# Where the sums of squares of x are made, and when their roots reach the tokens

## The chip, the cores and the metric

One core of a Trainium2 chip runs one program. The metric is the device time of one execution in microseconds (us), the lower the better. The engines have these short names: PE (TensorE, matrix products; PEld is its weight load), DVE (VectorE), ACT (ScalarE), POOL (GpSimd), SP (SyncE, which here issues most transfers). Results of PE land in PSUM, which has eight banks; everything else works in SBUF.

## The reference, cut to what matters

The kernel computes one decoder layer on 528 tokens (16 meta tokens and 512 of the sequence) of width 2048:

```
xn = x * rsqrt(mean(x * x) + eps) * g_pre        # one root for each token
p  = xn @ w_in                                   # q | k | v | z | r | h | b | c | z_conv
log_a = log_sigmoid(r @ w_gate_up + b_gate) / 16
y_gla  = rmsnorm(gated linear attention of q, k, v, log_a) * silu(z)
y_conv = b * conv3(c * h) * silu(z_conv)
out = x + rmsnorm(concat(y_gla, y_conv) @ w_out)
```

What the change concerns is the first line and the first columns of the second: q, k and r. The root of a token multiplies every column of that token, so a product may be made on x times g_pre alone, and its result multiplied by the root afterwards. The kernel calls the root's reciprocal `rstd` and keeps it spread over all 128 partitions, one column for each token.

## The kernel before, in words

Tokens are columns: x lies as 16 blocks (`kt`) of 128 features by 528 tokens, the tokens in two halves of 264 (8 meta tokens and 256 others each). A product in full fp32 accuracy is made of parts: each operand is split into a rounded high part and the low rest, and three matmuls (high by high, high by low, low by high) are added up in PSUM. ACT makes the high parts (a copy), DVE the low ones (a subtraction).

The kernel has these stages:

- **Load and first products.** x arrives in nine pieces (`XCUT`: two single blocks, then seven pairs). For each block ACT makes the high part (L670) and DVE the low part (L671), times g_pre. ACT also squares each piece. The first two squares go to the two planes of `acc`, the seven later pairs to one of two buffers `sqs`, and DVE adds them to `acc` (L696). Weights of k head 0 and q head 0 come in granules of eight blocks, split by L145 and L146. PE walks through the blocks: six matmuls for k, six for q (`plain_k`), four for r in each. Each of r, k and q has two banks, one for each half of the tokens.
- **rstd.** After step `kt == 10` in the code, PE adds the squares over partitions with a matrix of ones (fp32, two halves by two planes), which leaves the sum of each token on every partition. ACT takes the root (L711), DVE the reciprocal of 528 columns (L712). Then DVE scales r, k and q (`normal`, L723), and r is split into `rr` (L763 to L765), which the decay of head 0 and later ones reads.
- **Plain products** of v0, v1, z0 and z1 (`do_plain`), on x without its root, each 16 steps of six matmuls, two banks each, weights from three buffers for the high and three for the low parts. Beside them DVE makes `xn`, x times g_pre times rstd (`normalise`, L776, 16 instructions), and from it sums and differences of quarter blocks (`combine`, L783), split by L788 and L789 (`block`).
- **Fast products.** All other products go in pairs of column tiles by seven products of quarter blocks (`Pair`, order P5, P1, P6, P2, P3, P7, P4), with weights combined by L200 and L230 and split by L124 and L125, two ahead of PE. The attention's stages, the convolution and the output product follow in the same manner.

The order of the code is the order of priority: a planner walks through the code with its own costs, and puts an instruction into its engine's queue when its operands are ready by that reckoning, the earlier line first. Later lines can be drawn forward where an engine would have nothing to do. Each queue then runs strictly in that order on the chip.

The names that the text uses: `st` are the banks of the sums by ones, `warm` a bank that eight matmuls at the very start write and nobody reads, `scr` the tile that holds `acc`, `sqs` and small raw inputs, `ini` the pool of the first stage, `ident` a unit matrix, `HM` (after) the eight meta tokens of a half.

Of the kernel before, what the change touches and what calls it, by code (L numbers as in the profile page):

```python
# [9 lines left out]
F32 = mybir.dt.float32  # L10
F32R = mybir.dt.float32r
U32 = mybir.dt.uint32
AF = mybir.ActivationFunctionType
ALU = mybir.AluOpType

P = 128
D = 2048
KT = D // P
NM = 16
S = 512  # L20
L = NM + S
H = 4
DV = 256
RANK = 16
RU = 6 * RANK
HI = 4 * RANK
CH = 64
NP = S // P
# [3 lines left out]
XHALF = L // 2  # L32
# [13 lines left out]
def hymba_kernel(ctx, tc, xT, x, g_pre, w_r, w_t, w_up, b_gate, g_gla, w_conv, w_o, g_post, out):  # L46
# [10 lines left out]
    g1 = left.enter_context(tc.tile_pool(name="g1", bufs=1))  # L57

    def bank(name):
        return ps.tile([P, 512], F32, tag="bank", name=name)  # L60

    def mm(out_, lhsT, rhs, start, stop, **kw):
        nc.tensor.matmul(out_, lhsT, rhs, start=start, stop=stop, **kw)  # L63

    V, A, G = nc.vector, nc.scalar, nc.gpsimd


    epst = const.tile([P, 1], F32, name="epst")
# [13 lines left out]
    ones = const.tile([P, P], F32, name="ones")  # L82
    G.memset(ones, 1.0)
    ident = const.tile([P, P], F32, name="ident")
# [19 lines left out]
    scr = xp.tile([P, 3 * NB * XHALF], F32, tag="xt1", name="scr")  # L104
# [3 lines left out]
    WQ = 4 * NB * P  # L108
    wr2 = q0w[:, WQ:WQ + KT * 2 * RANK].rearrange("p (k r) -> p k r", r=2 * RANK)
    acc = scr[:, 0:2 * L].rearrange("p (k t) -> p k t", t=L)  # L110
    sqs = [scr[:, L * (2 + 2 * i):L * (4 + 2 * i)].rearrange("p (k t) -> p k t", t=L)
           for i in range(2)]
    wr_raw = scr[:, 6 * L:6 * L + KT * RANK].rearrange("p (k r) -> p k r", r=RANK)
    wup_raw = scr[0:RU, 7 * L:7 * L + H * P]
    r32 = scr[0:2 * RANK, 8 * L:9 * L]

    def raw_x(kt):
        return (xa if kt < NB else xb), kt % NB
# [13 lines left out]
    def new_raw(shape=None):  # L132
        tag = slots.pop(0)
        t = wp.tile(shape or [P, NB, P], F32, tag=tag, name="raw", bufs=1)
        held[id(t)] = (t, tag)
        return t

    def free(t):
        slots.append(held.pop(id(t))[1])
# [9 lines left out]
    def new_gran():  # L149
        return (wp.tile([P, NB, P], F32R, tag="whi", name="whi"),  # L150
                wp.tile([P, NB, P], F32R, tag="wlo", name="wlo"), new_raw())
# [5 lines left out]
        return gran  # L157


    def plain_k(pts, wt, kt, c0):  # L160
        hi, lo = wt[kt // NB][0:2]
        k = kt % NB
        first, last = kt == 0, kt == KT - 1
        xt, xk = raw_x(kt)
        w = XHALF - c0
        for n in range(2):
            mm(pts[n][:, 0:w], hi[:, k, :], xt[0][:, n, xk, c0:], first, False)
        for n in range(2):
            mm(pts[n][:, 0:w], hi[:, k, :], xt[1][:, n, xk, c0:], False, False)
        for n in range(2):  # L170
            mm(pts[n][:, 0:w], lo[:, k, :], xt[0][:, n, xk, c0:], False, last)

    def natural(t):

        return ([(t[:, NM // 2:NM // 2 + XHALF], 0, XHALF)],
                [(t[:, NM // 2 + XHALF:], NM // 2, XHALF), (t[:, 0:NM // 2], 0, NM // 2)])
# [473 lines left out]
    with tc.tile_pool(name="ini", bufs=1, reuse_waits="tile") as ini:  # L650
        tt = ini.tile([P, NB, XHALF], F32, name="tt")
        xr = ini.tile([P, KT, L], F32, name="xr")
        rstd = ini.tile([P, L], F32, name="rstd")

        warm = bank("warm")
        for _ in range(WARM):
            mm(warm[:, 0:P], ones, ones, True, True)
        r_ps = [bank("r0"), bank("r1")]
        k_ps = [bank("k00"), bank("k01")]
        q_ps = [bank("q00"), bank("q01")]  # L660
        q0v = q0w[:, 0:WQ].rearrange("p (g s k c) -> p g s k c", g=2, s=2, k=NB)
        wk = [new_gran(), None]
        wq_ = [(q0v[:, g, 0], q0v[:, g, 1], new_raw()) for g in range(2)]
        for n_, (k0, k1) in enumerate(XCUT):
            ks = slice(k0, k1)
            nc.sync.dma_start(xr[:, ks, :], xT[:, ks, :])
            for kt in range(k0, k1):
                xt, xk = raw_x(kt)
                src = xr[:, kt, :].rearrange("p (s t) -> p s t", t=XHALF)
                A.activation(xt[0][:, :, xk, :], src, AF.Copy, scale=gp[:, kt:kt + 1])  # L670
                V.scalar_tensor_tensor(out=xt[1][:, :, xk, :], in0=src, scalar=gp[:, kt:kt + 1],  # L671
                                       in1=xt[0][:, :, xk, :].bitcast(F32),
                                       op0=ALU.mult, op1=ALU.subtract)
            for a, b in WCUT.get(k0, ()):
                if a == NB:
                    free(wk[0][2])
                    wk[1] = new_gran()
                fill_gran(wk[a // NB], w_t[TILE["k0"]], a, b)
                fill_gran(wq_[a // NB], w_t[TILE["q0"]], a, b)
            if k0 == 0:  # L680
                A.dma_start(wr_raw, w_r)
                V.tensor_copy(wr2[:, :, 0:RANK], wr_raw)
                V.tensor_tensor(out=wr2[:, :, RANK:], in0=wr_raw,
                                in1=wr2[:, :, 0:RANK].bitcast(F32), op=ALU.subtract)
            if k0 == 8:
                nc.sync.dma_start(wup_raw, w_up)
                nc.sync.dma_start(bg, b_gate)
                G.tensor_scalar(out=nbg, in0=bg, scalar1=-1.0, scalar2=None, op0=ALU.mult)
                nc.sync.dma_start(gg, g_gla)
                nc.sync.dma_start(wc, w_conv)  # L690
            if k0 < 2:
                A.activation(acc[:, k0:k1, :], xr[:, ks, :], AF.Square)
            else:
                sq = sqs[n_ % 2]
                A.activation(sq, xr[:, ks, :], AF.Square)
                V.tensor_tensor(out=acc, in0=acc, in1=sq, op=ALU.add)  # L696
        for kt in range(KT):
            xt, xk = raw_x(kt)
            plain_k(k_ps, wk, kt, 0)
            plain_k(q_ps, wq_, kt, NM // 2)  # L700
            for i in range(2):
                for n in range(2):
                    mm(r_ps[n][0:2 * RANK, 0:XHALF], wr2[:, kt, :], xt[i][:, n, xk, :],
                       kt == 0 and i == 0, kt == KT - 1 and i == 1)
            if kt == 10:
                for n in range(2):
                    t = slice(n * XHALF, (n + 1) * XHALF)
                    st_ = bank(f"st{n}")
                    for i in range(2):
                        mm(st_[:, 0:XHALF], ones, acc[:, i, t], i == 0, i == 1)  # L710
                    A.activation(rstd[:, t], st_[:, 0:XHALF], AF.Sqrt, bias=epst, scale=1.0 / D)  # L711
                V.reciprocal(rstd, rstd)  # L712
        for raw in (wk[1][2], wq_[0][2], wq_[1][2]):
            free(raw)

# [3 lines left out]
                        op=ALU.subtract)  # L719
        def normal(dst, pts, c0, rows=slice(0, P)):  # L720
            for n in range(2):
                for o, s, e in dst[n]:
                    V.tensor_tensor(out=o, in0=pts[n][rows, s - c0:e - c0],  # L723
                                    in1=rstd[rows, n * XHALF + s:n * XHALF + e], op=ALU.mult)

        def new_k(h):
            kn[h] = g1.tile([P, L], F32, tag="kn", name="kn")
            return natural(kn[h])

        def new_q(h):  # L730
            qn[h] = g1.tile([P, L], F32, tag="qn", name="qn")[:, 0:S]
            return main_only(qn[h])
# [22 lines left out]
        def want_plain(n):  # L755
            if n in plain and n not in grans:
                grans[n] = [load_gran(n, g) for g in range(2)]

        want_plain("v0")

        normal(natural(r32), r_ps, 0, slice(0, 2 * RANK))
        rr = g1.tile([RU, L], F32R, tag="rr", name="rr")
        A.copy(rr[0:2 * RANK], r32)  # L763
        A.copy(rr[HI:RU], r32)
        V.tensor_tensor(out=rr[2 * RANK:HI], in0=r32, in1=rr[0:2 * RANK].bitcast(F32),  # L765
                        op=ALU.subtract)
        normal(new_k(0), k_ps, 0)
        normal(new_q(0), q_ps, NM // 2)

        xn = xr  # L770
        B = {(i, j): xn[:, NB * i:NB * i + NB, XHALF * j:XHALF * j + XHALF]
             for i in range(2) for j in range(2)}

        def normalise():
            for kt in range(KT):
# [16 lines left out]
        def do_plain(n, then):  # L792
            c0, new = plain[n]
            want_plain(n)
            if then:
                want_plain(then)
            pts = [bank(f"{n}{i}") for i in range(2)]
            for kt in range(KT):
                plain_k(pts, grans[n], kt, c0)
            grans.pop(n)  # L800
            normal(new(int(n[1:])), pts, c0)

# [4 lines left out]
        xt = [xp.tile([P, 3, NB, XHALF], F32R, tag=f"xt{i}", name=f"xt{i}") for i in range(2)]  # L807
# [23 lines left out]
        first = 3  # L831
# [14 lines left out]
    st = {}  # L846
# [223 lines left out]
```

## Time and profile before

| | |
|---|---|
| median of three runs | 819.46 us (818.55 to 820.85) |
| profiled execution | 820.74 us, span 819.0 us |
| granted TensorE clock, mean | 0.991 |
| PE busy | 793.0 us (97%), 6364 matmul instructions |
| DVE busy | 688.0 us (84%) |
| ACT busy | 437.2 us (53%) |
| POOL busy | 11.7 us (1%), 31 instructions |

The span is the time from the first to the last instruction of the profiled execution; its device time is 1.7 us longer. In the rows of the timeline the columns are: start, length (both in us), engine, line, operation, output and inputs by their names in the program, shape, number of instructions in the row, and in brackets the idle time before it with what ended it. A line is that of the helper which issues the instruction; all matmuls have line 63. Fp32 matmuls appear as two records each.

### The profile page before, as it was taken

Reading aid. Unit: us, or ns where it says so; the run is one execution under the profiler, and the core shown is the slowest. Engines: PE = TensorE matmul, PEld = TensorE weight load, DVE = VectorE, ACT = ScalarE, POOL = GpSimd, SP = SyncE. Lnnn points to the kernel's source line nnn. Section 1 sums busy time; section 2 is a strip of 40 time slices with the busy share of each in tenths; the row PEclk is TensorE's granted clock in tenths of the full one; section 3 lists DMA queues with packets and bytes.
Section 4 is the critical chain, followed back from the end, with each engine's and each line's share of the span. In section 5 each row is a group of like instructions: output and inputs, shape, how many; then the busy total and the mean of one; then the engine's idle time right before and its main releaser. Section 6 shows DMA issues by size and latency. Waiting matters only on the chain.

```text
span 819.0 us, 15183 instructions
## 1 busy us (share of the span) xinstructions
PE 793.0 (97%) x6364; PEld 775.8 (95%) x6364; DVE 688.0 (84%) x820; ACT 437.2 (53%) x638; POOL 11.7 (1%) x31
## 2 busy tenths in 40 slices
PE   8999999999999989999999999999999999999992
PEld 8999999999999989999999999999999889999992
DVE  6999979689796798878888878787879986788887
ACT  7635675585867475544444444444447534444442
POOL 0000000000000100000000000000000000000000
PEclk9999999999999999999999999999999999999997
DMA  9612242334224523153333333333333522333346
GB/s 290 222 52 92 93 134 97 104 109 150 76 79 145 164 79 104 69 189 112 119 104 111 104 112 107 111 106 115 102 110 119 171 78 77 103 103 107 100 166 248
DMA packets 33029, 98.99 MB, mean 121 GB/s; under 512 B 4064, under 2 KB 8800, under 8 KB 32320
## 3 DMA queue, kind: packets, MB, share of 16 engines
q1 hardware_dynamic: 28512, 88.44, 33.1%
q10 hardware_dynamic: 3168, 5.38, 1.9%
q0 software_dynamic: 1280, 4.20, 1.5%
q8 instruction: 50, 0.82, 0.4%
q14 instruction: 19, 0.16, 0.1%
HBM read 89.61 MB, written 8.39 MB: 120 GB/s over the span
## 4 chain that ended last, share of the span: by engine, by line
PE 76%; DVE 15%; ACT 3%; issue 3%; DMA 2%; DVEq 0%; SPq 0%; ACTq 0%
PE out L63 5%; PE out1P L63 4%; PE out2P L63 3%; PE out3P L63 3%; PE v L63 3%; DVE wlo L125 3%; PE h0c0P L63 2%; PE v2v3P L63 2%; PE h5c5P L63 2%; PE h2c2P L63 2%; PE h7c7P L63 2%; PE h6c6P L63 2%; PE h4c4P L63 2%; PE h3c3P L63 2%; PE h1c1P L63 2%
## 5 line engine op out<-in xcount | busy, mean ns | idle before, releaser
L124 ACT CAST whi<-raw 128x1024 fp32r<-128x1024 f32 x225 | 235.0, 1050 | 257.8 <-DVE raw L200 87.6
L125 DVE TENSOR_TENSOR wlo<-raw,whi 128x1024 fp32r<-128x1024 f32 x225 | 274.0, 1221 | 63.2 <-ACT whi L124 58.4
L200 DVE TENSOR_TENSOR raw<-raw 128x1024 f32<-128x1024 f32 x75 | 90.3, 1221 | 7.8 <-DMA raw<-in_w_t_dram 7.0
L230 DVE TENSOR_TENSOR raw<-raw 128x1024 f32<-128x1024 f32 x25 | 30.6, 1222 | 0.6
L145 ACT CAST whi<-raw 128x1024 fp32r<-128x1024 f32 (+2 forms) x13 | 10.9, 843 | 19.5 <-PE v L63 12.8
L63 PE MATMUL out<-whi,xt 128*128 128x512 f32 x64 | 20.0, 394 | 0.0
L63 PE MATMUL out3P<-whi,xt 128*128 128x256 f32 x96 | 17.2, 282 | 0.4 <-ACT whi L124 0.4
L63 PE MATMUL out2P<-whi,xt 128*128 128x256 f32 x96 | 17.2, 282 | 0.4 <-ACT whi L124 0.4
L63 PE MATMUL out1P<-whi,xt 128*128 128x256 f32 x96 | 17.1, 281 | 0.0
L63 PEld LDWEIGHTS out3P<-whi,xt 128*128 128x128 f32 x96 | 14.7, 188 | 0.6 <-ACT whi L124 0.6
L63 PEld LDWEIGHTS out2P<-whi,xt 128*128 128x128 f32 x96 | 14.7, 188 | 0.6 <-ACT whi L124 0.6
L63 PEld LDWEIGHTS out<-whi,xt 128*128 128x128 f32 x64 | 12.0, 188 | 2.8
L63 PEld LDWEIGHTS out1P<-whi,xt 128*128 128x128 f32 x96 | 14.7, 188 | 0.0
L63 PE MATMUL out2P<-wlo,xt 128*128 128x256 f32 x48 | 13.4, 280 | 0.0
L63 PE MATMUL out3P<-wlo,xt 128*128 128x256 f32 x48 | 13.4, 280 | 0.0
L63 PE MATMUL out1P<-wlo,xt 128*128 128x256 f32 x48 | 13.4, 280 | 0.0
L63 PE MATMUL out<-wlo,xt 128*128 128x512 f32 x32 | 12.6, 394 | 0.0
L146 DVE TENSOR_TENSOR wlo<-raw,whi 128x1024 fp32r<-128x1024 f32 (+2 forms) x13 | 12.5, 972 | 0.0
L605 DVE SCALAR_TENSOR_TENSOR y<-hh,wc,y 128x512 f32<-128x512 f32 x16 | 12.0, 749 | 0.2
L363 ACT ACTIVATE junk<-y 128x256 f32<-128x256 f32 x18 | 7.5, 418 | 8.7 <-DVE y L474 8.4
L63 PE MATMUL out3P<-whi,xb 128*128 128x256 f32 x64 | 11.7, 282 | 0.0
L63 PE MATMUL out2P<-whi,xb 128*128 128x256 f32 x64 | 11.6, 282 | 0.0
(751 smaller groups left out, 2708.8 us busy)
## 6 DMA issues: line engine op xcount, KB each, us to landing
raw<-in_w_t_dram SPq DMA_DIRECT2D x108, 512.0 KB, 4.0
raw<-in_w_o_dram SPq DMA_DIRECT2D x24, 512.0 KB, 4.0
raw<-in_w_o_dram SPq DMA_DIRECT2D x16, 256.0 KB, 3.6
xres<-in_x_dram SPq DMA_DIRECT2D x4, 1024.0 KB, 8.1
xr<-in_xT_dram SPq DMA_DIRECT2D x7, 528.0 KB, 7.3
z<-zd POOLq DMA_DIRECT2D x8, 256.0 KB, 3.5
yd<-z POOLq DMA_DIRECT2D x8, 256.0 KB, 2.5
yg<-yd SPq DMA_DIRECT2D x1, 2048.0 KB, 8.7
```

The costliest lines, as they stand in the source:

```text
L63: nc.tensor.matmul(out_, lhsT, rhs, start=start, stop=stop, **kw)
L124: A.copy(hi, raw)
L125: V.tensor_tensor(out=lo, in0=raw, in1=hi.bitcast(F32), op=ALU.subtract)
L145: A.copy(hi[:, k, :], raw[:, k, :])
L146: V.tensor_tensor(out=lo[:, k, :], in0=raw[:, k, :], in1=hi[:, k, :].bitcast(F32), op=ALU.subtract)
L200: V.tensor_tensor(out=a, in0=a, in1=b, op=ALU.add)
L230: V.tensor_tensor(out=raw["11"], in0=raw["11"], in1=raw["22"], op=ALU.subtract)
L363: A.activation(junk, oy["src"], AF.Square, accum_out=fin["ssq"][:, t, n:n + 1])
L605: V.scalar_tensor_tensor(out=y, in0=hh[:, i:i + S], scalar=wc[:, j, i:i + 1], in1=y, op0=ALU.mult, op1=ALU.add)
```

## The change

The sums of squares of five of the seven later pairs are added by GpSimd; those of the last two pairs and the two planes are added by DVE, so that one plane is left. A third buffer of squares is there. The roots are no longer made on 128 equal partitions: the squares of 128 tokens are the weights of a matmul with one column of ones, which leaves one sum per token on its own partition (four groups of 128 tokens, two of 8 meta tokens). Root and reciprocal are taken of these six columns, a unit matrix is scaled by them, and a matmul of ones with that diagonal spreads them over all partitions. All of it goes through the bank `warm`. The sums stand in the code after step 3 of v0, the spread after step 8, and scaling r, k and q behind it; splitting r stands after step 1 of v1. In the loop over blocks r goes ahead of k and q, and the two halves of q share a bank.

```diff
-    sqs = [scr[:, L * (2 + 2 * i):L * (4 + 2 * i)].rearrange("p (k t) -> p k t", t=L)
-           for i in range(2)]
+    sqs = [scr[:, L * i:L * (2 + i)].rearrange("p (k t) -> p k t", t=L) for i in (2, 4, 9)]
...
-    def plain_k(pts, wt, kt, c0):
+    def plain_k(pts, wt, kt, c0, shared=False):
...
+        kw = [{}, {"skip_group_check": True} if shared else {}]
         for n in range(2):
-            mm(pts[n][:, 0:w], hi[:, k, :], xt[0][:, n, xk, c0:], first, False)
+            mm(pts[n][:, 0:w], hi[:, k, :], xt[0][:, n, xk, c0:],
+               first and not (shared and n), False, **kw[n])
...
-        q_ps = [bank("q00"), bank("q01")]
+        q_bank = bank("q0")
+        q_ps = [q_bank[:, 0:S // 2], q_bank[:, S // 2:]]
...
-                sq = sqs[n_ % 2]
+                sq = sqs[n_ % 3]
                 A.activation(sq, xr[:, ks, :], AF.Square)
-                V.tensor_tensor(out=acc, in0=acc, in1=sq, op=ALU.add)
+                if k0 < 12:
+                    G.tensor_tensor(out=acc, in0=acc, in1=sq, op=ALU.add)
+                elif k0 == 14:
+                    V.tensor_tensor(out=sq, in0=sq, in1=sqs[(n_ - 1) % 3], op=ALU.add)
+                    V.tensor_tensor(out=acc, in0=acc, in1=sq, op=ALU.add)
+                    V.tensor_tensor(out=acc[:, 0, :], in0=acc[:, 0, :], in1=acc[:, 1, :],
+                                    op=ALU.add)
         for kt in range(KT):
             xt, xk = raw_x(kt)
-            plain_k(k_ps, wk, kt, 0)
-            plain_k(q_ps, wq_, kt, NM // 2)
             for i in range(2):
                 for n in range(2):
                     mm(r_ps[n][0:2 * RANK, 0:XHALF], wr2[:, kt, :], xt[i][:, n, xk, :],
                        kt == 0 and i == 0, kt == KT - 1 and i == 1)
-            if kt == 10:
-                for n in range(2):
-                    t = slice(n * XHALF, (n + 1) * XHALF)
-                    st_ = bank(f"st{n}")
-                    for i in range(2):
-                        mm(st_[:, 0:XHALF], ones, acc[:, i, t], i == 0, i == 1)
-                    A.activation(rstd[:, t], st_[:, 0:XHALF], AF.Sqrt, bias=epst, scale=1.0 / D)
-                V.reciprocal(rstd, rstd)
+            plain_k(k_ps, wk, kt, 0)
+            plain_k(q_ps, wq_, kt, NM // 2, True)
+        HM = NM // 2
+        inv = ini.tile([P, NP + 2], F32, name="inv")
+        diag = ini.tile([P, NP, P], F32, name="diag")
+        diam = ini.tile([HM, 2, HM], F32, name="diam")
+        col = [n * XHALF + HM + t * P for n in range(2) for t in range(2)]
+
+        def token_sums():
+            o = warm[:, 0:NP + 2]
+            for t in range(NP):
+                mm(o[:, t:t + 1], acc[:, 0, col[t]:col[t] + P], ones[:, 0:1], True, True)
+            for n in range(2):
+                mm(o[0:HM, NP + n:NP + n + 1], acc[:, 0, n * XHALF:n * XHALF + HM], ones[:, 0:1],
+                   True, True)
+            for p_, c_ in ((slice(0, P), slice(0, NP)), (slice(0, HM), slice(NP, NP + 2))):
+                A.activation(inv[p_, c_], o[p_, c_], AF.Sqrt, bias=epst[p_], scale=1.0 / D)
+                V.reciprocal(inv[p_, c_], inv[p_, c_])
+            for t in range(NP):
+                A.activation(diag[:, t, :], ident, AF.Copy, scale=inv[:, t:t + 1])
+            for n in range(2):
+                A.activation(diam[:, n, :], ident[0:HM, 0:HM], AF.Copy,
+                             scale=inv[0:HM, NP + n:NP + n + 1])
+
+        def spread():
+            r_ = rstd.rearrange("p (n t) -> p n t", t=XHALF)
+            for t in range(NP):
+                mm(warm[:, t * P:(t + 1) * P], ones, diag[:, t, :], True, True)
+            A.copy(r_[:, :, HM:], warm.rearrange("p (n t) -> p n t", n=2))
+            for n in range(2):
+                mm(warm[:, n * HM:(n + 1) * HM], ones[0:HM], diam[:, n, :], True, True)
+            A.copy(r_[:, :, 0:HM], warm[:, 0:NM].rearrange("p (n t) -> p n t", n=2))
...
-        normal(natural(r32), r_ps, 0, slice(0, 2 * RANK))
-        rr = g1.tile([RU, L], F32R, tag="rr", name="rr")
-        A.copy(rr[0:2 * RANK], r32)
...
-        normal(new_k(0), k_ps, 0)
-        normal(new_q(0), q_ps, NM // 2)
...
+        def first_results():
+            normal(natural(r32), r_ps, 0, slice(0, 2 * RANK))
+            normal(new_k(0), k_ps, 0)
+            normal(new_q(0), q_ps, NM // 2)
+
+        def r_parts():
+            A.copy(rr[0:2 * RANK], r32)
+            A.copy(rr[HI:RU], r32)
+            V.tensor_tensor(out=rr[2 * RANK:HI], in0=r32, in1=rr[0:2 * RANK].bitcast(F32),
+                            op=ALU.subtract)
...
             for kt in range(KT):
                 plain_k(pts, grans[n], kt, c0)
+                if n == "v0" and kt == 3:
+                    token_sums()
+                if n == "v0" and kt == 8:
+                    spread()
+                    first_results()
+                if n == "v1" and kt == 1:
+                    r_parts()
```

More of the change, by code (lines that the diff above doesn't have):

```diff
@@ L165, in plain_k @@
         w = XHALF - c0
+        kw = [{}, {"skip_group_check": True} if shared else {}]
         for n in range(2):
-            mm(pts[n][:, 0:w], hi[:, k, :], xt[0][:, n, xk, c0:], first, False)
+            mm(pts[n][:, 0:w], hi[:, k, :], xt[0][:, n, xk, c0:],
+               first and not (shared and n), False, **kw[n])
         for n in range(2):
-            mm(pts[n][:, 0:w], hi[:, k, :], xt[1][:, n, xk, c0:], False, False)
+            mm(pts[n][:, 0:w], hi[:, k, :], xt[1][:, n, xk, c0:], False, False, **kw[n])
         for n in range(2):
-            mm(pts[n][:, 0:w], lo[:, k, :], xt[0][:, n, xk, c0:], False, last)
+            mm(pts[n][:, 0:w], lo[:, k, :], xt[0][:, n, xk, c0:], False, last, **kw[n])
     def natural(t):
@@ L757, in want_plain @@
                 grans[n] = [load_gran(n, g) for g in range(2)]
-        want_plain("v0")
-        normal(natural(r32), r_ps, 0, slice(0, 2 * RANK))
-        rr = g1.tile([RU, L], F32R, tag="rr", name="rr")
-        A.copy(rr[0:2 * RANK], r32)
-        A.copy(rr[HI:RU], r32)
-        V.tensor_tensor(out=rr[2 * RANK:HI], in0=r32, in1=rr[0:2 * RANK].bitcast(F32),
-                        op=ALU.subtract)
-        normal(new_k(0), k_ps, 0)
-        normal(new_q(0), q_ps, NM // 2)
         xn = xr
@@ L772, in hymba_kernel @@
              for i in range(2) for j in range(2)}
+        rr = g1.tile([RU, L], F32R, tag="rr", name="rr")
+        def first_results():
[7 more added lines that the diff above has]
+                            op=ALU.subtract)
         def normalise():
```

## The prediction

> **What bounds the kernel now.** I read the page first, then the waits of TensorE, then the windows and timelines of the first 105 us, the only stretch that the change touches.
>
> ```profile
> span 819.0 us, 15183 instructions
> PE 793.0 (97%) x6364; PEld 775.8 (95%) x6364; DVE 688.0 (84%) x820; ACT 437.2 (53%) x638; POOL 11.7 (1%) x31
> ```
>
> ```profile
> PE z2z3P L63 <- DVE wlo L125: 0.8, 1, 0.8
> PE st L63 <- DVE scr L696: 0.2, 1, 0.2
> ```
>
> PE is the bound, so only two things count: what PE issues, and what makes it wait. The windows (columns: stretch, its length, busy PE, PEld, DVE, ACT, POOL, clock, DMA share, GB/s) show that DVE is the second bound here:
>
> ```profile
> 20.00:25.00 5.00, 5.00 (x44) 4.89 (x42) 5.00 (x7) 4.96 (x8) 0.54 (x1) 1.00 1.00 374
> 45.00:50.00 5.00, 5.00 (x43) 5.00 (x42) 5.00 (x8) 1.05 (x1) 0.00 (x0) 1.00 0.06 23
> 90.00:95.00 5.00, 4.23 (x36) 4.03 (x35) 5.00 (x5) 1.39 (x3) 0.00 (x0) 1.00 0.55 186
> 95.00:100.00 5.00, 4.87 (x41) 4.67 (x41) 5.00 (x7) 3.15 (x4) 0.00 (x0) 1.00 0.04 6
> ```
>
> DVE has no idle time in these windows, and at 90 to 100 us PE loses 0.77 + 0.13 us to it. So from `normalise` (L776) to the weights of product P3, DVE is one unbroken chain whose end PE already waits for. DVE's own timeline has the places that matter:
>
> ```profile
> 21.83 1.44 DVE L671 SCALAR_TENSOR_TENSOR xb<-xr,gp,xb 128x528 fp32r<-128x528 f32 x2
> 35.52 3.45 DVE L712 RECIPROCAL rstd<-rstd 128x528 f32<-128x528 f32 x1 [0.38 <-ACT rstd L711]
> 39.07 0.84 DVE L723 TENSOR_TENSOR kn<-k,rstd 128x264 f32<-128x264 f32 x3
> 41.23 1.20 DVE L146 TENSOR_TENSOR wlo<-raw,whi 128x1024 fp32r<-128x1024 f32 x1
> 42.47 0.70 DVE L765 TENSOR_TENSOR rr<-scr,rr 32x528 fp32r<-32x528 f32 x1
> 43.18 4.16 DVE L776 SCALAR_TENSOR_TENSOR xr<-xr,gp,rstd 128x528 f32<-128x528 f32 x6
> 47.26 1.22 DVE L146 TENSOR_TENSOR wlo<-raw,whi 128x1024 fp32r<-128x1024 f32 x1
> 84.03 2.42 DVE L789 TENSOR_TENSOR xa<-tt,xa 128x1056 fp32r<-128x1056 f32 x2
> 96.58 1.22 DVE L230 TENSOR_TENSOR raw<-raw 128x1024 f32<-128x1024 f32 x1
> 97.71 1.22 DVE L125 TENSOR_TENSOR wlo<-raw,whi 128x1024 fp32r<-128x1024 f32 x1
> ```
>
> **The change, part by part.** *TensorE, removed.* The four fp32 column sums on `ones` stand in eight records between the low parts of k:
>
> ```profile
> 32.47 0.28 PE L63 MATMUL k<-xb,wlo 128*128 128x264 f32 x1
> 32.92 2.05 PE L63 MATMUL st<-scr,ones 128*128 128x264 f32 x8 [0.17 <-DVE scr L696]
> 34.61 0.48 PE L63 MATMUL k<-xb,wlo 128*128 128x264 f32 x1
> ```
>
> The next k matmul came 2.14 us after the last one, where its neighbours are 0.12 us apart: 2.02 us go, wait included.
>
> *TensorE, added.* Six sums with the squares as weights and one column moving, two records each; four spreads of 128 columns; two small ones. The trace has no one-column matmul. The nearest fp32 rows are the scores:
>
> ```profile
> 133.75 0.83 PE L63 MATMUL sc<-eqk 128*128 128x128 f32 x6
> 134.51 0.68 PE L63 MATMUL sc<-esx 128*64 128x64 f32 x8
> 135.12 0.51 PE L63 MATMUL v2v3P<-xa,whi 128*128 128x264 f32 x2
> ```
>
> Start to start that is 0.76/6 = 0.127 us a record for 128 columns and 0.61/8 = 0.076 for 64. The sums' 12 records cost 0.9 to 1.5 us; I take 1.3, since a full 128-column weight must be loaded. The spread's 8 records cost 1.0 and its 4 small ones 0.3 at 0.076. Together 2.6 (2.2 to 2.8) against 2.02: by itself PE is 0.6 us longer. Two halves of q in one bank cost nothing, if one bank is as fast as two: z goes to two banks, z2z3P to one.
>
> ```profile
> 83.95 0.64 PE L63 MATMUL z<-xb,whi 128*128 128x256 f32 x4
> 84.43 0.40 PE L63 MATMUL z<-xb,wlo 128*128 128x256 f32 x2
> ...
> 88.22 0.40 PE L63 MATMUL z2z3P<-xt,whi 128*128 128x256 f32 x2
> 88.46 0.28 PE L63 MATMUL z2z3P<-xt,wlo 128*128 128x256 f32 x1
> ```
>
> Both go on at 0.12 us a matmul (0.48/4 and 0.24/2). Putting r ahead of k and q keeps the number of matmuls.
>
> *DVE before rstd.* Seven adds of 1.25 us and the 3.45 us reciprocal leave; two adds, half an add (0.7) and two reciprocals of a few columns return. Some 9 us are freed ahead of 43 us. Nothing of it reaches PE at once: PE is busy all through (the window at 20), and what DVE can do next is either behind rstd or behind a weight buffer. Only one piece moves forward, the split of v1's second half (47.26), which waits for v0's first half alone.
>
> *rstd comes later.* This is the step that decides. The order of a queue follows the order of the code, later code being drawn forward only where the engine would wait. PE never waits here, so the sums run after four steps of v0 and the spread after nine.
>
> ```profile
> 39.96 0.65 PE L63 MATMUL v<-xa,whi 128*128 128x264 f32 x4
> 45.82 0.66 PE L63 MATMUL v<-xb,whi 128*128 128x264 f32 x4
> ```
>
> Eight steps of v0 take 5.86 us, 0.733 each. v0 starts at 39.96 - 2.02 = 37.9. The spread starts at 37.9 + 9 x 0.733 + 1.3 = 45.8 and ends at 47.0. Roots, reciprocals and diagonals have 45.8 - 42.2 = 3.6 us for some 2 us of ACT work in which ACT idles otherwise, so PE doesn't wait for them. ACT's copy of 512 columns out of PSUM is not in the trace; 264 and 384 columns are:
>
> ```profile
> 111.37 0.37 ACT L268 COPY f<-k1q1P 128x264 f32<-128x264 f32 x1
> 128.61 0.47 ACT L849 CAST kt<-tpk 128x384 fp32r<-128x384 f32 x1
> ```
>
> 0.1 us for 120 more columns gives 0.58; the copy ends at 47.6, the small one for the meta tokens at about 48.1. Then DVE scales r, k and q (39.07 to 41.23: 2.16 us before), now ahead of `normalise` in the code; q needs no meta column and starts at 47.6. `normalise` starts near 49.9 instead of 43.18: 6.7 us late. (In a row of DVE work an instruction counts 0.08 less than its length, as the next starts before its end: six of L776 take 4.08 us from 43.18 to 47.26, 0.68 each.) The chain behind it loses 1.14 (v1's split, done before) and gains 0.62 (L765 is now written after it): 6.2 us late. At P3's weights the subtraction for P7 (L230, 1.14) stands ahead today and would stand behind in code order, which gives back 1.0: 5.2 us. PE's new wait is all of that, because its wait there is already above zero; its own 0.6 disappears inside.
>
> Bounds of the 5.2: if the order also puts off P4's block (84.03, two halves, 2.3 us), which PE needs last, 2.9 remain; if nothing is reordered and the copies wait behind a weight cast of 1.05 us, 7.3.
>
> Later waits don't pay it back: the raw weight buffers are freed by the same DVE chain, so the loads shift with it. The banks are full (warm, r, k, q, v0 hold eight) but v1 needs two only at 52 us, when the spread's bank and r's are free.
>
> *GpSimd's five adds.* POOL has no two-input row. From below stands a memset of half the width, from above its fixed part:
>
> ```profile
> 1.73 0.53 POOL L94 MEMSET keep<- 128x528 f32 x1
> 22.14 0.54 POOL L688 TENSOR_SCALAR nbg<-bg 128x4 f32<-128x4 f32 x1 [19.68 <-DMA bg<-in_b_gate_dram]
> ```
>
> The adds' own spacing is in the group of DVE's (min, median, max ns; first and last start):
>
> ```profile
> L696 DVE TENSOR_TENSOR scr<-scr x7: 1250/1255/1259, 13.2 to 31.6; 128x1056 f32<-128x1056 f32 x7
> ```
>
> A POOL add takes 1.06 us if it runs like a memset; 0.5 + 3 x 1.06 = 3.7 if two reads and a write take turns. I take the middle, 2.4: five adds, one for each 3.07 us (13.2 to 31.6 in six steps), keep up, and the sums are ready by about 36, before PE wants them at 40.9. By this estimate they cost nothing. [...]
>
> **The rivals.**
> (a) *POOL and DVE exclude each other while both read two operands.* For it: nearly all DVE work between 13 and 32 us has two SBUF inputs. Against it: while L688 ran, L671 beside it kept its length, but that POOL instruction has only one input. Without its add DVE is busy 3.07 - 1.25 = 1.8 us a period; 2.4 of POOL make 4.2, so each period slips 1.1. Steps 12 and 13:
>
> ```profile
> 25.67 1.35 ACT L670 ACTIVATE xb<-xr,gp 128x528 fp32r<-128x528 f32 x2
> ...
> 30.06 0.64 PE L63 MATMUL k<-xb,whi 128*128 128x264 f32 x4
> ```
>
> ACT has their high parts at 27.0, DVE the low ones 1.4 later at 28.4; behind four slips that is 32.8, and PE wants them at 30.1. It waits 2.7 us, everything behind shifts, and the time is 819.5 + 5.2 + 2.7 = 827.4. [...]
>
> (b) *Not slower: the sums and the spread are drawn forward into the k loop.* Code is drawn forward today:
>
> ```profile
> 22.16 0.61 ACT L716 CAST wup<-scr 64x512 fp32r<-64x512 f32 x1
> 23.42 1.36 ACT L670 ACTIVATE xb<-xr,gp 128x528 fp32r<-128x528 f32 x2
> ```
>
> L716 is written behind the loop and runs ahead of L670's fifth pair. If the planner sees PE waiting for low parts, it could put the sums at 36 and the spread near 39; rstd is there at 41, `normalise` starts at 43 or before. The point from which this decides is a start by about 44: then the freed DVE time also removes the 0.9 us of waits, PE adds 0.6, and the time is about 819. Against it: matmuls of k and q are always ready by 30 us, and `st`, written at step 10, went later (step 13) and not earlier.
>
> (c) *The DVE order recovers most of it*, P4's block and L230 both put off: 819.5 + 2.9 = 822.4. It lies in the forecast's own range.
>
> **How the numbers follow.** The profiled execution took 820.74 us around its 819.0 us span; the median is 819.46, which I use as base: 819.46 + 5.2 = 824.7. Chances: forecast with (c) 0.50 (own range 822 to 827), (a) 0.25, (b) 0.20, unforeseen 0.05. The range reaches from below (b) to above (a) with its 7.3 bound partly in: 818.5 to 829.5. What a measurement can tell from no change is about 0.3%, 2.5 us. Slower is the forecast and (a), nearly whole: 0.73; (b) lies around zero, so same 0.15; faster 0.12.
>
> **What would show it.** In the changed kernel: no `st` rows, v0 starting near 38; a group of one-column matmuls near 41 and the spread near 46; L776's successor starting near 50; no DVE idle from there to 105; PE idle of some 6 us between 86 and 105 on wlo and on the low parts of the blocks, against 0.9 now; and the same pattern from then on, shifted. (a) would show as DVE instructions of over 2 us between 13 and 30 and PE waiting on xb. The forecast is wrong if `normalise` starts by 44, or if it starts at 50 and PE's waits before 105 stay under 2 us; then DVE's chain had slack that I don't see.

## The result and the profile after

The changed kernel takes 834.02 us (median of 5 runs, 833.58 to 836.23) against 819.46 us: 14.6 us more, a ratio of 1.018 with a 95% interval of 1.0165 to 1.0194. The time lies outside the predicted range, in the direction that was forecast. The profiled execution has a span of 831.3 us, 12.3 more than before; it is the fastest of its five, and the one of the kernel before was slower than its median, so the spans lie closer together than the medians.

The head of the page of the changed kernel, and its windows (columns as before: stretch, length, busy PE, PEld, DVE, ACT, POOL, clock, DMA share, GB/s):

```profile
span 831.3 us, 15224 instructions
PE 797.7 (96%) x6380; PEld 779.2 (94%) x6380; DVE 690.6 (83%) x817; ACT 438.7 (53%) x646; POOL 25.7 (3%) x36
```

```profile
15.00:20.00 5.00, 5.00 (x43) 4.64 (x42) 5.00 (x4) 5.00 (x8) 3.62 (x3) 1.00 1.06 310
20.00:25.00 5.00, 2.01 (x13) 1.71 (x11) 5.00 (x4) 4.90 (x8) 5.00 (x3) 0.88 0.96 382
25.00:30.00 5.00, 3.93 (x25) 3.43 (x23) 5.00 (x3) 5.00 (x8) 4.12 (x2) 0.78 0.43 139
40.00:45.00 5.00, 5.00 (x44) 4.89 (x43) 1.25 (x2) 0.21 (x1) 0.00 (x0) 1.00 0.55 189
95.00:100.00 5.00, 3.85 (x28) 3.50 (x29) 5.00 (x7) 5.00 (x6) 0.00 (x0) 1.00 0.14 52
100.00:110.00 10.00, 7.86 (x51) 7.45 (x50) 10.00 (x10) 2.59 (x5) 0.53 (x1) 0.83 0.31 107
```

Two stretches have lost PE time, and they belong to two different steps of the change. At 20 to 30 us, where PE had no idle time before, it is busy 5.94 of 10 us, and DVE, "busy" throughout, completes 4 and 3 instructions per window, where it completed 7 in the window from 20 to 25 before. At 95 to 110 us PE waits behind a DVE that never rests, though DVE had been nearly idle at 40 to 45 us. The waits of PE in the first 130 us name both:

```profile
PE z2z3P L63 <- ACT whi L123: 3.8, 4, 1.4
PE r L63 <- DVE xa L674: 3.0, 1, 3.0
PE r L63 <- DVE q0w L686: 1.8, 1, 1.8
PE r L63 <- DVE xb L674: 1.6, 1, 1.6
...
PE z2z3P L63 <- DVE wlo L124: 0.8, 1, 0.8
```

The first row is DVE's lateness too: the casts wait there for sums of weights (L202) that DVE makes. By the page PE's idle time has grown by 7.6 us (819.0 - 793.0 = 26.0 before, 831.3 - 797.7 = 33.6 after) and its busy time by 4.7; of the latter an estimated 3 us are the clock, worked out from the windows (0.88 and 0.78 at 20 to 30 us, 0.83 at 100 to 110). Here is what happens at 13 to 30 us, POOL's adds first and DVE's rows beside them:

```profile
13.26 2.49 POOL L700 TENSOR_TENSOR scr<-scr 128x1056 f32<-128x1056 f32 x1 [10.80 <-ACT scr L698]
16.59 2.73 POOL L700 TENSOR_TENSOR scr<-scr 128x1056 f32<-128x1056 f32 x1 [0.85 <-ACT scr L698]
19.86 2.89 POOL L700 TENSOR_TENSOR scr<-scr 128x1056 f32<-128x1056 f32 x1 [0.53 <-ACT scr L698]
...
23.38 5.83 POOL L700 TENSOR_TENSOR scr<-scr 128x1056 f32<-128x1056 f32 x2
```

```profile
13.83 3.16 DVE L674 SCALAR_TENSOR_TENSOR xa<-xr,gp,xa 128x528 fp32r<-128x528 f32 x2 [0.92 <-ACT xa L673]
16.91 2.96 DVE L145 TENSOR_TENSOR wlo<-raw,whi 128x512 fp32r<-128x512 f32 x1
19.80 0.68 DVE L145 TENSOR_TENSOR q0w<-raw,q0w 128x512 fp32r<-128x512 f32 x1
20.40 3.60 DVE L674 SCALAR_TENSOR_TENSOR xa<-xr,gp,xa 128x528 fp32r<-128x528 f32 x2
23.92 2.96 DVE L145 TENSOR_TENSOR wlo<-raw,whi 128x512 fp32r<-128x512 f32 x1
26.80 2.96 DVE L145 TENSOR_TENSOR q0w<-raw,q0w 128x512 fp32r<-128x512 f32 x1
29.68 1.44 DVE L674 SCALAR_TENSOR_TENSOR xb<-xr,gp,xb 128x528 fp32r<-128x528 f32 x2
```

The same DVE instruction takes 0.68 us at 19.80, where it begins just ahead of an add, and 2.96 at 16.91, where an add is under way. The add there ends at 16.59 + 2.73 = 19.32 and the DVE instruction at 19.87, 0.55 later, which is little less than its usual length: by these times it got little or nothing done before POOL's add had ended. Each add costs DVE one such hold: 3.16 - 1.44 = 1.7, then 2.3, 2.2, 2.3 and 2.3, together 10.7 us, in exchange for 6.3 us of adds that it no longer does. All five fall ahead of the low parts of step 8 (xb), which DVE makes at 29.68 instead of 21.83. PE stands still for 2.99 us at 20 us and for 1.56 at 28.9, with a slow clock between:

```profile
23.37 0.43 PE L63 MATMUL r<-xa,q0w 128*32 128x264 f32 x2 [2.99 <-DVE xa L674]
...
24.81 1.48 PE L63 MATMUL q<-xa,q0w 128*128 128x256 f32 x6
```

v0 and `normalise` then start here:

```profile
45.55 0.64 PE L63 MATMUL v<-xa,whi 128*128 128x264 f32 x4
```

```profile
45.87 1.23 DVE L145 TENSOR_TENSOR wlo<-raw,whi 128x1024 fp32r<-128x1024 f32 x1 [4.62 <-ACT whi L144]
49.93 0.29 DVE L733 RECIPROCAL inv<-inv 128x4 f32<-128x4 f32 x2 [2.83 <-ACT inv L732]
53.62 1.23 DVE L145 TENSOR_TENSOR wlo<-raw,whi 128x1024 fp32r<-128x1024 f32 x1 [3.40 <-ACT whi L144]
...
57.70 2.10 DVE L815 SCALAR_TENSOR_TENSOR xr<-xr,gp,rstd 128x528 f32<-128x528 f32 x3
...
112.32 1.22 DVE L124 TENSOR_TENSOR wlo<-raw,whi 128x1024 fp32r<-128x1024 f32 x1
```

`normalise` starts at 57.70 instead of 43.18, 14.5 us late; P3's weights are split at 112.32 instead of 97.71, 14.6 late. The chain between the two has lost nothing and won nothing: in this kernel its end moves with its start. From there the shift stays: v6v7P starts at 296.0 (281.5 before). Then some 2.5 us come back, as h0c0P starts at 318.2 instead of 306.2. PE's waits between 270 and 330, first before and then after the change:

```profile
PE v6v7P L63 <- DVE wlo L125: 2.4, 1, 2.4
```

```profile
PE v6v7P L63 <- DVE wlo L124: 1.2, 1, 1.2
```

Half of the return is this wait. The other half is the clock: in the kernel before it falls behind the wait, as its window shows, and in the changed kernel the window behind the shorter wait (310 to 315) has 1.00.

```profile
295.00:300.00 5.00, 3.76 (x19) 3.76 (x20) 5.00 (x10) 3.98 (x8) 0.00 (x0) 0.66 0.34 105
```

With 2.5 of 14.5 returned the span is 12.3 longer. All runs below that build on the changed kernel wait 1.2 us here, on time or late. Of those that build on the kernel before, the one with GpSimd's adds alone is 7.2 us late here and still waits 1.9; only the one with idle one-input work waits 1.2. So the return seems to go with the changed code and not with the delay; why isn't shown.

### The profile page after: what moved, and what is told of

Its sections match the earlier page's. It is cut to its first block, busy times and chain, and to the rows that moved or that the text cites. A ratio compares the mean times of both kernels' runs of the same rounds, so it can differ in the third digit from the quotient of the medians.

```text
span 831.3 us, 15224 instructions
## 1 busy us (share of the span) xinstructions
PE 797.7 (96%) x6380; PEld 779.2 (94%) x6380; DVE 690.6 (83%) x817; ACT 438.7 (53%) x646; POOL 25.7 (3%) x36
## 4 chain that ended last, share of the span: by engine, by line
PE 75%; DVE 15%; ACT 4%; DMA 3%; issue 2%; SPq 0%; DVEq 0%; ACTq 0%
PE out L63 5%; PE out3P L63 4%; PE out1P L63 4%; PE out2P L63 3%; DVE wlo L124 3%; PE k3q3P L63 2%; PE v2v3P L63 2%; PE h0c0P L63 2%; PE h7c7P L63 2%; PE h6c6P L63 2%; PE h5c5P L63 2%; PE h4c4P L63 2%; PE h3c3P L63 2%; PE h2c2P L63 2%; PE b6s6P L63 2%; PE b5s5P L63 2%
## 5 line engine op out<-in xcount | busy, mean ns | idle before, releaser
L202 DVE TENSOR_TENSOR raw<-raw 128x1024 f32<-128x1024 f32 x75 | 90.4, 1222 | 6.4 <-DMA raw<-in_w_t_dram 5.6
L232 DVE TENSOR_TENSOR raw<-raw 128x1024 f32<-128x1024 f32 x25 | 30.6, 1222 | 0.6
L145 DVE TENSOR_TENSOR wlo<-raw,whi 128x1024 fp32r<-128x1024 f32 (+2 forms) x13 | 17.0, 1324 | 8.0 <-ACT whi L144 8.0
L674 DVE SCALAR_TENSOR_TENSOR xa<-xr,gp,xa 128x528 fp32r<-128x528 f32 x8 | 9.7, 1248 | 7.1 <-ACT xa L673 7.1
L700 POOL TENSOR_TENSOR scr<-scr 128x1056 f32<-128x1056 f32 x5 | 13.9, 2772 | 12.3 <-ACT scr L698 12.2
L63 PE MATMUL z2z3P<-xt,whi 128*128 128x256 f32 x48 | 10.7, 318 | 3.4 <-ACT whi L123 3.4
L63 PEld LDWEIGHTS z2z3P<-xt,whi 128*128 128x128 f32 x48 | 8.7, 221 | 4.0 <-ACT whi L123 4.0
```

Of the source, the lines that this page charges most:

```text
L145: V.tensor_tensor(out=lo[:, k, :], in0=raw[:, k, :], in1=hi[:, k, :].bitcast(F32), op=ALU.subtract)
L202: V.tensor_tensor(out=a, in0=a, in1=b, op=ALU.add)
L232: V.tensor_tensor(out=raw["11"], in0=raw["11"], in1=raw["22"], op=ALU.subtract)
L700: G.tensor_tensor(out=acc, in0=acc, in1=sq, op=ALU.add)
```

## The experiments

Theory A was read from these rows: the loss is the sum of GpSimd's adds, which hold VectorE, and of rstd's late place; r ahead of k and q was thought to add 1.5. Theory B: all of it is GpSimd's. Theory C: GpSimd costs nothing, all of it is the late rstd. Unless an edit says otherwise, nothing is left out of the computation.

**Adds back on VectorE** (`e1_v_adds`), on the changed kernel:

```diff
                 if k0 < 12:
-                    G.tensor_tensor(out=acc, in0=acc, in1=sq, op=ALU.add)
+                    V.tensor_tensor(out=acc, in0=acc, in1=sq, op=ALU.add)
```

> The changed kernel with its five GpSimd adds on VectorE; all else as changed. Theory A (the loss has three parts: r ahead of k and q 1.5 us, GpSimd's adds holding VectorE's two-input instructions 6.1 us, rstd after nine steps of v0 some 7 us): v0 starts near 39.4 instead of 45.6, no VectorE row of twice its usual length before 32 us, normalise starts near 51.6, time 826 to 828. Theory B (the whole loss is GpSimd's and rstd's lateness is free): 819 to 821. Theory C (GpSimd's adds cost nothing, all of it is the late rstd): 833 to 835.

Measured: 828.18 us, ratio to before 1.0104 (1.008 to 1.0128). PE loses nothing in this run's window from 20 to 25 us, and in its DVE timeline `normalise` starts earlier:

```profile
20.00:25.00 5.00, 5.00 (x44) 4.87 (x42) 5.00 (x7) 4.96 (x8) 1.70 (x1) 1.00 1.03 406
```

```profile
53.20 2.11 DVE L815 SCALAR_TENSOR_TENSOR xr<-xr,gp,rstd 128x528 f32<-128x528 f32 x3
```

5.8 us of the loss go with GpSimd's adds and 8.7 stay (the interval is some 2 us either way): 0.2 above A's range, and neither B nor C. v0 started at 41.05, not at the expected 39.4 (39.96 before); this run waited 2.9 us for r's low weights at its start, the changed kernel 1.8.

**The sums and the spread earlier** (`e4_v_adds_early`), on the run above:

```diff
         for kt in range(KT):
...
+            if kt == 13:
+                token_sums()
+            if kt == 15:
+                spread()
...
+        want_plain("v0")
+        first_results()
+        r_parts()
...
-                if n == "v0" and kt == 3:
-                    token_sums()
-                if n == "v0" and kt == 8:
-                    spread()
-                    first_results()
-                if n == "v1" and kt == 1:
-                    r_parts()
```

> As the run before (adds on VectorE, r first, q in one bank), but the sums stand after step 13 of the loop over blocks, the spread after step 15, and r, k and q are scaled before v0. Against the run before only the time at which rstd is there differs. Theory A: normalise starts by 43 us, the time is 818 to 821, some 7 us under the run before. Theory B: no difference from the run before beyond 1 us.

Measured: 821.72 us, ratio 1.0025 (1.0015 to 1.0034), that is 6.5 us under the run before.

DVE's timeline of this run at the first row of `normalise`:

```profile
45.55 3.49 DVE L821 SCALAR_TENSOR_TENSOR xr<-xr,gp,rstd 128x528 f32<-128x528 f32 x5
```

`normalise` starts at 45.55 instead of 53.20. Moved 7.7 us, it carries the end with it by 6.5. That is the late rstd by itself, and A's second part stands. It started later than the expected 43, and the time is 0.7 above the stated range: the spread follows step 15 and PE takes it in that order.

**GpSimd's adds alone** (`e2_pool_alone`), on the kernel before, with the third buffer of squares:

```diff
-                V.tensor_tensor(out=acc, in0=acc, in1=sq, op=ALU.add)
+                (G if k0 < 12 else V).tensor_tensor(out=acc, in0=acc, in1=sq, op=ALU.add)
```

> The kernel before with only its first five adds of squares moved to GpSimd (and the third buffer of squares). Theory A: VectorE's instructions beside an add take 2 us longer, PE waits for xa and xb as in the changed kernel, v0 starts 5 to 7 us later than the 40.0 us of before, and the time is 825 to 828. Theory B: 832 to 835. Theory C: 819 to 820.

Measured: 828.19 us, ratio 1.0112 (1.0085 to 1.0139): 8.6 us for this one part, 0.2 above A's range, with an interval of some 2 us either way. v0 starts at 47.39, 7.4 us late where 5 to 7 were expected. PE's waits at its first products in this run:

```profile
PE k L63 <- DVE xa L670: 4.8, 3, 2.9
PE k L63 <- DVE xb L670: 1.5, 1, 1.5
```

Together with the 6.5 of the late rstd that is 15.1, close to the 14.6 of the whole change. The two parts add up because they lie one behind the other: GpSimd's holds delay PE's way to v0, and the late place of rstd delays `normalise` from v0's start on. That second stretch is the same with five adds on GpSimd (57.70 - 45.55 = 12.15 us) and with none (53.20 - 41.05 = 12.15).

**The diagonal roots alone, r last** (`e6_v_early_rlast`): the run with early roots, with

```diff
-            for i in range(2):
-                for n in range(2):
-                    mm(r_ps[n][0:2 * RANK, 0:XHALF], wr2[:, kt, :], xt[i][:, n, xk, :],
-                       kt == 0 and i == 0, kt == KT - 1 and i == 1)
             plain_k(k_ps, wk, kt, 0)
             plain_k(q_ps, wq_, kt, NM // 2, True)
+            for i in range(2):
+                for n in range(2):
+                    mm(r_ps[n][0:2 * RANK, 0:XHALF], wr2[:, kt, :], xt[i][:, n, xk, :],
+                       kt == 0 and i == 0, kt == KT - 1 and i == 1)
```

> The diagonal roots alone: adds on VectorE, sums after step 13, spread after step 15, and r after k and q as before. Against the run with r first only the order of r differs. Theory A: 1 to 1.5 us under that run, 817 to 820, at or a little below the kernel before, since VectorE is rid of the 3.45 us reciprocal. If r's order costs nothing, the two are equal within 0.5 us.

Measured: 820.24 us, ratio 1.0007 (0.9998 to 1.0017). r's place is worth the expected 1.5 us here (the time itself is 0.2 above the expected range), and what remains of the change (diagonal roots, one bank for q) is no gain and no loss that can be told from zero. Taken off in this order, GpSimd's adds, the late rstd, r's place and the rest are 5.8, 6.5, 1.5 and 0.6 us; r's place counts only once GpSimd's adds are gone, as the next run shows.

**r last in the changed kernel** (`e3_r_last`): the same edit of the order, all else as changed.

> The changed kernel with r after k and q in each step, as before the change; all else as changed. Theory A (r ahead costs 1.5 us at the start, where r's low weights come last, and all behind shifts): PE's 1.8 us wait for q0w is gone, 832 to 833. If VectorE is the bound from 13 us on whatever PE does first: 834, no difference.

Measured: 835.51 us, ratio 1.0195 (1.017 to 1.0219). The 1.5 us do not come back, so r's place is no term of the 14.6: where DVE, held by POOL, is the bound from 13 us on, PE's late start is covered. With r last the parts that were measured alone add up: 8.6 + 6.5 + 0.6 = 15.7, against 835.51 - 819.74 = 15.8. By the profile this kernel is even later, v0 at 47.01. Its PE waits are longer (4.7 us for xa, 3.0 for xb), and the clock falls only after the last of them, as its windows show:

```profile
25.00:30.00 5.00, 2.20 (x19) 1.95 (x17) 5.00 (x3) 5.00 (x8) 3.87 (x2) 1.00 0.49 155
30.00:35.00 5.00, 4.77 (x27) 4.58 (x28) 4.94 (x8) 1.64 (x2) 0.00 (x0) 0.66 0.51 188
```

In the changed kernel the slow stretch (0.88 and 0.78, at 20 to 30) lies ahead of another wait that covers it; here nothing follows that would. That this makes the 1.5 us between the two medians is argued, not shown, and their intervals overlap.

**Two adds instead of five on GpSimd** (`e11_two_pool_adds`), on the changed kernel: `(G if k0 < 6 else V)` in place of `G`.

> The changed kernel with two of the five adds on GpSimd (the first two pairs), three on VectorE. Theory A (each GpSimd add holds VectorE some 2.2 us): between the 828.2 of none and the 834.0 of five, at 829 to 831. If only the last adds, which meet the x parts that PE waits for, did the harm: 828.

Measured: 829.01 us, ratio 1.0108 (1.0092 to 1.0123), 0.8 above none, less than the intervals can tell from zero, and 5.0 below five. Its two adds hold DVE by the same 1.7 and 2.3 us (3.15 for the first pair, 2.96 for a split), yet cost nearly nothing: PE has no wait for xa or xb in this run, so at 13 to 19 us its operands are still ahead of it. The price isn't linear in the adds (0.8 us for two, 5.8 for five); here it begins when DVE's lead over PE on the low parts is used up.

**Idle GpSimd work beside the kernel before.** Three runs of one execution each have the kernel before with work on GpSimd that nobody uses, on a free part of `scr`; the adds stay on VectorE.

```diff
                 V.tensor_tensor(out=acc, in0=acc, in1=sq, op=ALU.add)
+                if k0 < 12:
+                    G.tensor_tensor(out=dum, in0=xr[:, ks, :], in1=xr[:, ks, :], op=ALU.add)
+                    # second run: G.tensor_scalar(out=dum, in0=xr[:, ks, :], scalar1=1.0,
+                    #                             scalar2=None, op0=ALU.mult)
+                    # third run:  G.memset(dum, 1.0)
```

> The kernel before, its adds kept on VectorE, with five idle two-input adds on GpSimd beside them (result not used, nothing waits for them). If the collision is at the ports, VectorE's rows beside them grow by 2 us each, as in the changed kernel, and the time rises by 5 to 10 us. If the loss in the changed kernel came from waiting for the sums, no row grows and the time is 819 to 821.

Measured with two inputs: 830.81 us (one run), 11 above before and 1 above the expected 5 to 10. Nothing waits for these adds, so it is GpSimd's work beside VectorE's and not the sums coming late; where on the chip the two collide no run shows. POOL's timeline of this run and, below, DVE's:

```profile
13.32 2.33 POOL L699 TENSOR_TENSOR scr<-xr 128x1056 f32<-128x1056 f32 x1 [1.25 <-DMA xr<-in_xT_dram]
15.93 2.07 POOL L699 TENSOR_TENSOR scr<-xr 128x1056 f32<-128x1056 f32 x1 [0.28 <-DMA xr<-in_xT_dram]
```

```profile
13.77 2.43 DVE L146 TENSOR_TENSOR q0w<-raw,q0w 128x512 fp32r<-128x512 f32 x1
16.12 3.00 DVE L697 TENSOR_TENSOR scr<-scr 128x1056 f32<-128x1056 f32 x1
```

0.68 has become 2.43 and 1.25 has become 3.00. Both end after the add beside them (these end at 15.65 and 18.00), 0.55 and 1.12 us after.

> The kernel before, its adds kept on VectorE, with five idle copies on GpSimd beside them (one input of 128x1056 read, result not used). If any GpSimd read of SBUF holds VectorE's second input, VectorE's rows beside them grow by the length of the copy (some 1 to 1.5 us each) and the time rises by 3 to 7 us; if only a two-input instruction does, 819 to 820.

Measured with one input: 822.08 us (one run), 2.4 above the 819.74 of before, below the expected 3 to 7. POOL and DVE again:

```profile
13.43 6.28 POOL L699 TENSOR_SCALAR scr<-xr 128x1056 f32<-128x1056 f32 x2 [1.44 <-DMA xr<-in_xT_dram]
```

```profile
13.59 2.01 DVE L697 TENSOR_TENSOR scr<-scr 128x1056 f32<-128x1056 f32 x1 [0.30 <-ACT scr L696]
15.53 1.43 DVE L672 SCALAR_TENSOR_TENSOR xa<-xr,gp,xa 128x528 fp32r<-128x528 f32 x2
16.88 1.55 DVE L146 TENSOR_TENSOR wlo<-raw,whi 128x512 fp32r<-128x512 f32 x1
```

The copy takes longer than an add (3.1 us), but DVE is held for only 0.8 to 0.9 us of it (2.01 for 1.25, 1.55 for 0.68) and takes its usual time in the rest (1.43 for the two that make xa; 1.44 in the kernel before).

> The kernel before, its adds kept on VectorE, with five memsets of 128x1056 on GpSimd beside them, which read nothing. If reads are what collides, VectorE's rows keep their length and the time is 818 to 821; if any GpSimd work collides, they grow by about 1 us each.

Measured with memsets: 821.08 us (one run). The planner put them at 2.2 to 7.4 us, since they wait for nothing, so the run says nothing on 13 to 30 us. But some DVE work ran beside them, as POOL's row and DVE's show, with the last one's counterpart in the kernel before at the end:

```profile
3.24 4.11 POOL L699 MEMSET scr<- 128x1056 f32 x4
```

```profile
4.65 0.77 DVE L672 SCALAR_TENSOR_TENSOR xa<-xr,gp,xa 128x528 fp32r<-128x528 f32 x1 [4.65 <-ACT xa L671]
5.34 0.42 DVE L146 TENSOR_TENSOR wlo<-raw,whi 128x256 fp32r<-128x256 f32 x1
5.67 0.76 DVE L683 CAST q0w<-scr 128x256 fp32r<-128x256 f32 x1
```

```profile
5.97 0.28 DVE L682 CAST q0w<-scr 128x256 fp32r<-128x256 f32 x1
```

The instructions with two inputs keep their 0.77 and 0.42; the cast takes 0.76 instead of 0.28.

**One bank for q alone** (`e5_q_bank`), on the kernel before: the bank `q0` and `plain_k`'s `shared`, as in the change.

> The kernel before with only the two halves of q in one bank. Every theory: 819 to 820, no difference; if two accumulations in one bank slowed PE, 16 steps of 0.71 us for q would grow.

Measured: 820.29 us, ratio 0.9999 (0.9988 to 1.001). No cost, as taken.

**The roots as early as they can be** (`e10_early_two_planes`): the run with r last, its adds as before the change, the sums over both planes, one step earlier each:

```diff
-                mm(o[:, t:t + 1], acc[:, 0, col[t]:col[t] + P], ones[:, 0:1], True, True)
+                for i in range(2):
+                    mm(o[:, t:t + 1], acc[:, i, col[t]:col[t] + P], ones[:, 0:1], i == 0, i == 1)
...
-            if kt == 13:
+            if kt == 12:
                 token_sums()
-            if kt == 15:
+            if kt == 14:
                 spread()
```

> The diagonal roots as early as they can be: adds of all seven pairs on VectorE in the order of before, the sums taken over both planes (twelve matmuls) after step 12, the spread after step 14, r after k and q. Theory A (normalise's start decides by how much VectorE's chain ends late): normalise starts at 40 to 43 us instead of 45.2 in the later version, PE's waits for z2z3P fall under 0.9 us, time 818 to 819.7: even with before or just below. If it stays at 820.2, the chain is held by something other than rstd.

Measured: 822.4 us, ratio 1.0028 (1.0017 to 1.004), and `normalise` at 48.18. The expectation failed, for a reason that PE's timeline in this run and the window from 35 to 40 (clock third from the end) show:

```profile
33.98 2.22 PE L63 MATMUL warm<-ones,scr 128*128 128x1 f32 x24 [0.60 <-DVE scr L699]
36.13 0.40 PE L63 MATMUL k<-xb,wlo 128*128 128x264 f32 x1
36.37 0.87 PE L63 MATMUL q<-xb,q0w 128*128 128x256 f32 x6
...
38.86 1.48 PE L63 MATMUL q<-xb,q0w 128*128 128x256 f32 x6
```

```profile
35.00:40.00 5.00, 5.00 (x40) 4.91 (x40) 1.50 (x4) 2.06 (x8) 0.00 (x0) 0.76 0.50 144
```

After 0.60 us of waiting and 2.2 us of one-column matmuls the clock fell to 0.76, and q's six matmuls took 1.48 us instead of 0.87. The sums over two planes also take 1 us longer than those over one (2.22 us against 1.23 in the run with r last and early roots). The spread came at 41.0 and everything behind it late: v0 at 44.56 instead of 40.43 in the run with r last and early roots, `normalise` 3.0 us later than there, and the time 2.2 us longer, which fits A. The profiled execution is the slowest of this run's six, so its clock need not stand for all of them. No version here beats the kernel before.

## Why the prediction was wrong

The direction and the mechanism that was thought likeliest held; the size did not, for one term that was set to nothing.

- **GpSimd's five adds, "By this estimate they cost nothing": the step that failed.** The add's own price was right (2.4 taken, 2.49 to 2.9 measured). The error lay in asking only whether POOL keeps up, and leaving what POOL does to DVE to a rival with a chance of 0.25. It costs 5.8 us in the changed kernel and 8.6 alone. With two inputs on both sides a DVE split took 2.96 us and ended 0.55 us after the add beside it; alone it takes 0.68.
- **Rival (a) had the mechanism and 2.7 us for it, too little.** Its 1.1 us net for each add is near what was measured: 10.7 us of holds less 6.3 us of adds, over five, is 0.9. What it had wrong is where they fall. It spread the slips over 13 to 32 us, one for each pair of blocks, and first saw PE wait at step 12; all five holds came ahead of step 8's low parts, and PE waited at step 6 and again at step 8. The rival's own signs all came: DVE rows of over 2 us between 13 and 30, PE waiting on xb. It left out the clock, too: behind the 2.99 us wait six matmuls of q took 1.48 us instead of 0.87.
- **rstd later, "This is the step that decides": right.** From v0's start to `normalise`: 49.9 - 37.9 = 12.0 predicted, 57.70 - 45.55 = 12.15 measured. Its price was put at 5.2, with 7.3 as the upper bound; measured alone it is 6.5. PE's waits for z2z3P were to be some 6 us: in the run with the adds on VectorE they are 5.9 (5.1 for the casts, 0.8 for the low parts). Behind them that run's clock falls to 0.74 (110 to 115 us), which the sum didn't have. The piece of v1's split that was to move ahead did so (53.62), DVE's freed time stands as a gap at 41 to 54 us, and no later wait swallowed it. The 1 us that L230 was to give back didn't come: in the changed kernel its successor L232 still stands ahead of P3's split, at 111.19, where code order would have put it behind.
- **v0's start, predicted 37.9, was 45.55.** With the adds on VectorE it is 41.05, of which 2.9 are PE's wait for r's low weights; the rest, 38.1, says that the term for the removed sums by ones was about right. What was missing is GpSimd, and r's place where nothing covers it.
- **r ahead of k and q was called free by counting matmuls.** It costs 1.5 us where PE is the bound at the start, because r's low weights come last; under GpSimd's holds it cost nothing. The right answer in this kernel came from the wrong reason.
- **"Later waits don't pay it back": right for the delay.** 2.5 us came back at 282 to 306 us, but as much (2.4) also in the run with early roots and r last, which had no late rstd to pay back.
- **One bank for q: free, as taken.** The sums cost PE 1.05 us (48.48 to 49.53, 12 records) against 1.3 taken.
- **(b) and (c) did not occur.** The sums stood behind four steps of v0, as written, and DVE's order ahead of P3 recovered nothing.

## What to carry to other kernels

Work given to GpSimd was not free for VectorE here: each two-input add of 2.5 to 2.9 us held it for 1.7 to 2.3 us. Before moving such work, look whether it and the VectorE instructions beside it read two SBUF operands each. If they do, reckon with holds of this size until a run shows otherwise, and ask which operands that puts off and how far ahead of their reader they are. Relief on an engine is worth something only if it comes before the operand that starts that engine's next chain; ask first when that operand will be there. And ask of two delays whether they lie one behind the other, as GpSimd's holds and the late rstd, which added up, or before the same wait, as r's place and GpSimd's holds, where one covered the other.

## What the runs showed of the hardware that was not expected

- A GpSimd instruction with one input (128x1056) ran 3.1 us, and two-input work of VectorE beside it took at most 0.9 us longer (2.01 us for 1.25, 1.55 for 0.68), less than a third of the copy. Beside one with two inputs, of 2.33 and 2.07 us, it ended 0.55 and 1.12 us after the add, little less than the 0.68 and 1.25 that it takes alone.
- Beside memsets on GpSimd (1.0 us each) two-input work kept its 0.77 and 0.42 us, but one cast took 0.76 instead of 0.28. This is one cast in one execution; why isn't shown.
- One-column matmuls may not keep TensorE's clock up: in one execution 24 records in 2.2 us, behind a wait of 0.6, were followed by matmuls at 0.6 of the usual speed (six of q in 1.48 us instead of 0.87, granted clock 0.76 at 35 to 40 us). Twelve such records in 1.05 us in the changed kernel, without a wait, were not (granted clock 1.00 in that window and the next). That the records had a part in it is argued from this, not shown.
- A lower granted clock came behind a wait of 2.99 us in the changed kernel (0.88 and 0.78 at 20 to 30 us) and behind one of 2.42 in the kernel before (0.66 at 295 to 300; the wait began at 294 us). The length of the wait alone doesn't decide in these runs: in the changed kernel with r last one of 2.90 us, at 20 us, was followed by a clock of 1.00.
